# Gates of six column tiles by Strassen's form in a stage of their own, for all tokens

## The chip, the cores and the metric

The kernel runs on one core of a Trainium2 chip. A core has TensorE (PE, matrix products into PSUM banks), VectorE (DVE), ScalarE (ACT), GpSimd (POOL), SyncE (SP, which only issues DMAs here) and 16 DMA engines. The metric is the device time of one execution in microseconds (us); less is better.

## The reference

One encoder layer over 1024 tokens of width 1024, in fp32. Cut to what matters:

```python
mod = jax.nn.silu(c) @ w_ada + b_ada                      # six vectors of 1024
h = rmsnorm(x, norm1_g) * (1.0 + sc1) + sh1
z = h @ w_in
u, v, q, k, va, gate_a, gate_b = jnp.split(z, cuts, axis=-1)
a_out = gmlp_branch(u, v, gm_v_g, gm_w_s, gm_b_s) @ w_a   # 512 -> 1024
b_out = window_attention_branch(q, k, va, q_norm_g, k_norm_g, attn_sink) @ w_b
merged = jax.nn.sigmoid(gate_a) * a_out + jax.nn.sigmoid(gate_b) * b_out
x = x + gt1 * (merged @ w_o)
h2 = rmsnorm(x, norm2_g) * (1.0 + sc2) + sh2
f_gate, f_up = jnp.split(h2 @ w_ffn_in, 2, axis=-1)
x = x + gt2 * ((jax.nn.silu(f_gate) * f_up) @ w_ffn_out)
```

`gate_a` and `gate_b` are 1024 columns each of `h @ w_in`: the change is about these two products.

## The kernel before

**Products.** Matmuls take operands of type F32R; to keep fp32 accuracy every operand is split into a high and a low part, and every product is three matmuls (`mm3`: high x high, high x low, low x high) that accumulate in a PSUM bank of 128 x 512. A weight unit is 128 x 1024: `raw_unit` loads it (512 KB), `unit` casts it to `wh` on ScalarE and subtracts to `wl` on VectorE. `raw`, `wh` and `wl` have three buffers each.

**Stages.** Activations are held transposed (columns on partitions, tokens along the row), eight column tiles `d` or `k` of 128. Tokens run in two halves of 512: `half(0)`, `half(1)`. A half makes q and k (with `h`, the normalised input, of eight tiles), v, the attention with fillers between its steps (u and the gates of tiles 0 and 1), the spatial gating, and then two loops over `d`:

- The tile loop: the gates of tile `d` (for `d` > 1: two units `w_gb[d]`, `w_ga[d]`, 24 matmuls each), the projections of both branches with `w_ab[d]` (2 x 12 matmuls), sigmoid by tanh on ScalarE, the gated sum on VectorE and its split into `mH`, `mL`. Beside it run dot products for the conditioning vectors (`ada_next`: a `w_ada` unit of 512 KB times `silu_c` on VectorE with a sum, 1024 wide), and in half 0 loads of half 1's x with squares and their sum (`sumsq`), from which `col_rstd` takes the norms by four matmuls with ones.
- The output projection: 24 matmuls per tile with `w_o[d]`, the residual, x1 stored to `x1d`. In half 0 it also modulates x of half 1 to the `h` of half 1 (`h_next`), in half 1 x1 of half 0 to `h2`.

After both halves comes the FFN, already by Strassen's form, with an order written out by hand.

**What sets the order.** The Tile scheduler places instructions on each engine by their dependences; where `in_order[0]` is set they keep the program's order. Loads from SP (`load`) always keep the program's order among themselves, so a load that waits for its buffer holds all later loads. Stores go out on POOL's queue (`store`). Every operation of an engine is recorded at the helper's line L75; loads at L127, stores at L130.

**Buffers.** `stream("hs")` and `stream("xs")` are 128 x 512 with two buffers each; `midt` is 128 x 2048 with eight; `hid` 128 x 2048 with four; PSUM has four `mm` and four `at` banks.

Of the kernel before, what the change touches and what calls it, by code (L numbers as in the profile page):

```python
# [38 lines left out]
def kernel(  # L39
    ctx: ExitStack,  # L40
    tc: tile.TileContext,
    xT: bass.AP,
    c: bass.AP,
    cols: bass.AP,
# [47 lines left out]
    dram = ctx.enter_context(tc.tile_pool(name="dram", bufs=1, space=bass.MemoryType.DRAM))  # L92
    psum = ctx.enter_context(pool("psum", 4, space=PSUM))

    n_names = [0]
# [22 lines left out]
    def hid():  # L118
        return hpool.tile([P, 2048], F32R, tag="h", name=nm("h")).rearrange(
            "p (a b) -> p a b", a=4  # L120
        )

# [101 lines left out]


    apool_ctx = ExitStack()
    apool = apool_ctx.enter_context(pool("apool"))
    attp = apool_ctx.enter_context(pool("attp", 6))

    silu_c = apool.tile([P, D], F32, tag="silu_c", name="silu_c")  # L230
    rows = apool.tile([P, GW + 2 * HD + NH], F32, tag="rows", name="rows")
# [234 lines left out]

    EARLY = 6
    firsts, raw2 = {}, []
    ffn_ctx = ExitStack()
    fps = []  # L470

    def open_ffn():

        apool_ctx.close()
        fp = ffn_ctx.enter_context(pool("ffn"))
        fps.append(fp)
        for part in range(2):
            t = fp.tile([P, 2048], F32R, tag=f"b22{'hl'[part]}", name=nm("first"))
            firsts[part] = t

# [21 lines left out]

    def ada_next(n):
        for _ in range(n):
            if ada_queue:
                col, gain = ada_queue.pop(0)
                ada_dot(raw_unit(w_ada2[col - GT1]), col)
                ada_end(col, gain)

    def x_rows(hf, k):  # L510
        return xT[k * P : (k + 1) * P, hf * HALF : (hf + 1) * HALF]

    def half(hf):
# [62 lines left out]
        for k in range(KT):  # L576
            if hf == 0:
# [22 lines left out]
            elif k == 0:  # L600
                wq, wk = early.pop(0), early.pop(0)
            if k == 4:
                wk = unit(w_kv[1], V)
            if k % 2 == 1 and k < KT - 1:
                wq_next = unit(w_q[(k + 1) // 2], V)
            sts = [(hH[k // 4][:, k % 4, t * P : (t + 1) * P], hL[k // 4][:, k % 4, t * P : (t + 1) * P])
                   for t in range(NT)]
# [6 lines left out]
            for group in ((q_parts, k_parts) if k == 4 else (q_parts + k_parts,)):  # L614
                for e in range(2):
                    for ps, st, w, o, n, first, last in group:
                        if e == 0:
                            T.matmul(ps, st[0], w[0][:, o : o + n], start=k == 0 and first, stop=False)
                            T.matmul(ps, st[0], w[1][:, o : o + n], start=False, stop=False)
                        else:  # L620
                            T.matmul(ps, st[1], w[0][:, o : o + n], start=False,
                                     stop=bool(k == KT - 1 and last))
            if k % 2 == 1 and k < KT - 1:
                wq = wq_next
        in_order[0] = False
        if hf == 0:
            attention_constants()
        else:
            col_rstd(sums[0], NT, rcol[2])
        vts = {}  # L630
# [90 lines left out]


        vps = [mm_bank() for _ in range(NT)]
        wvs.append(unit(w_v[1], V))
# [64 lines left out]
        for s in range(nw):  # L789
            if s:  # L790
# [3 lines left out]
                den = exps(*sc, work[s][1])  # L794
            fill(FA)
            normalise(sc[0], sc[2], den)
            if s == 0:
# [60 lines left out]
        for ct in range(4):  # L858
# [3 lines left out]
            split(pt, gH[:, ct, :], gL[:, ct, :])  # L862

        mH = [None, None]
        mL = [None, None]
        for d in range(KT):
            if d % 4 == 0:
                mH[d // 4] = midt(F32R, 4)  # L870
                mL[d // 4] = midt(F32R, 4)
            ms = []
            in_order[0] = d < 2
            if d > 1:
                wg2 = unit(w_gb[d])
                wab = unit(w_ab[d])
                wg1 = unit(w_ga[d])
            else:
# [12 lines left out]
            split(ms[0], mH[d // 4][:, d % 4, :], mL[d // 4][:, d % 4, :])  # L891
            in_order[0] = False
            if d > 1:
                ada_next(2 + hf)
            if hf == 0:
                xk = stream("hs")
                load(xk, x_rows(1, d))
                if d == 0:
                    ssn = ss_tile()[:, :HALF]
                in_order[0] = d == 0  # L900
                sumsq(xk, d == 0, ssn)
                in_order[0] = False
        if hf == 0:
            col_rstd(ssn, NT, rcol[1])


        if hf == 1:
            assert not ada_queue
            open_ffn()
        dst = [[hid(), hid()], [hid(), hid()]]  # L910
        if hf == 0:
            h_next.extend(dst)
        else:
            h2[0] = dst
            x1B.extend([midt(F32, 4), midt(F32, 4)])
            h2m.extend([midt(F32, 4), midt(F32, 4)])
        ss = ss_tile()[:, :HALF]
        wo_next = unit(w_o[0])
        for d in range(KT):
            wo = wo_next  # L920
            if d < KT - 1:
                wo_next = unit(w_o[d + 1])
            elif hf == 0:
                early.extend([unit(w_q[0], V), unit(w_kv[0], V)])
            else:
                raw1 = raw_unit(w_gate[1])
                raw2.append(raw_unit(w_gate[2]))
# [3 lines left out]
            if hf == 1 and d in (2, 4):  # L931
                early.append(first_unit(d // 2 - 1))
            if hf == 0 and d in (2, 5):
                ada_next(1)
            xk = stream("hs")
            load(xk, x_rows(1, d) if hf == 0 else x1d[d * P : (d + 1) * P, :HALF])
            xr = stream("xs")
            load(xr, x_rows(hf, d))
            pw = mm_bank()
            for k in range(KT):  # L940
                kc = slice(k * P, (k + 1) * P)
                mm3(pw, (wo[0][:, kc], wo[1][:, kc]),
                    (mH[k // 4][:, k % 4, :], mL[k // 4][:, k % 4, :]), k == 0, k == KT - 1)
            if d == 0:
                rb = spread(rcol[1 + hf], NT)
            hi, lo = (t[d // 4][:, d % 4, :] for t in dst)
            modulate(xk, rb, d, SC1 if hf == 0 else SC2, SH1 if hf == 0 else SH2, hi, lo,
                     xk if hf == 0 else h2m[d // 4][:, d % 4, :])
            x1 = tmp() if hf == 0 else x1B[d // 4][:, d % 4, :]
            V.scalar_tensor_tensor(out=x1, in0=pw, scalar=mod[:, GT1 + d : GT1 + d + 1], in1=xr,  # L950
                                   op0=ALU.mult, op1=ALU.add)
            sumsq(x1, d == 0, ss)
            store(x1d[d * P : (d + 1) * P, hf * HALF : (hf + 1) * HALF], x1)
            if hf == 1 and d == KT - 1:
                early.append(unit(None, V, raw1))
        in_order[0] = False
        sums.append(ss)

    half(0)
    half(1)  # L960

    fp = fps[0]
    Q = HALF  # L970

    def fpt(name):
        return fp.tile([P, 2048], F32R, tag=name, name=nm(name)).rearrange("p (a b) -> p a b", a=4)

# [306 lines left out]
    with tc.manual_schedule():  # L1281
        U[4, 0], U[5, 0], U[0, 0], U[1, 0] = early
        buf = mid.tile([P, 2048], F32, tag="mid", name=nm("ws"))
        ws, ups = buf[:, :UNIT], (buf[:, UNIT:], fp.tile([P, UNIT], F32, tag="ru", name="ru"))
        g3 = gate_raw(3)
# [172 lines left out]
def _layout(inputs):  # L1458
# [10 lines left out]
    def col(v):  # L1469
# [9 lines left out]
    out = {  # L1479
        "xT": xt,  # L1480
        "c": a["c"][0],
        "cols": np.concatenate([col(a["b_ada"][0]), col(a["norm1_g"][0]), col(a["norm2_g"][0]),
# [39 lines left out]
```

## Time and profile before

| | us |
|---|---|
| median of three runs (lowest, highest) | 1257.36 (1256.26, 1259.01) |
| the profiled execution: span from first to last instruction | 1255.1 |
| TensorE busy in it | 1234.1 |
| VectorE, ScalarE, POOL busy | 861.5, 543.5, 132.7 |
| DMA queue of SP, of POOL | 155.59 MB, 57.68 MB |

The median lies 2.3 above the profiled span; the profiled execution's time beyond its span is not listed apart. Busy times are per engine and overlap. Rows of groups give the operation, output and inputs by the program's names, the shape, a count, the busy time, the mean in ns, and the idle time ahead of them with what ended it. A group's mean is the time from start to end of one instruction; in a dense row the next starts earlier, so prices are read from starts.

### The profile page before, as it was taken

Reading aid. Unit: us, or ns where it says so; the run is one execution under the profiler, and the core shown is the slowest. Engines: PE = TensorE matmul, PEld = TensorE weight load, DVE = VectorE, ACT = ScalarE, POOL = GpSimd, SP = SyncE. Lnnn points to the kernel's source line nnn. Section 1 sums busy time; section 2 is a strip of 40 time slices with the busy share of each in tenths; the row PEclk is TensorE's granted clock in tenths of the full one; section 3 lists DMA queues with packets and bytes.
Section 4 is the critical chain, followed back from the end, with each engine's and each line's share of the span. In section 5 each row is a group of like instructions: output and inputs, shape, how many; then the busy total and the mean of one; then the engine's idle time right before and its main releaser. Section 6 shows DMA issues by size and latency. Waiting matters only on the chain.

```text
span 1255.1 us, 15405 instructions
## 1 busy us (share of the span) xinstructions
PE 1234.1 (98%) x5714; PEld 1025.1 (82%) x5714; DVE 861.5 (69%) x1404; ACT 543.5 (43%) x867; POOL 132.7 (11%) x148
## 2 busy tenths in 40 slices
PE   5999999999999999999999999999999999999998
PEld 4888888888888888888888888888888887888887
DVE  8998875557468786666698766666666666455646
ACT  5467853334257772334454333333333334433342
POOL 0123310000032330000100000001010000010001
PEclk9999999999999999999999999999999999999999
DMA  9422145546522126665712454464554449896652
GB/s 362 169 84 67 52 143 184 177 159 211 197 70 67 51 89 196 201 194 209 250 36 102 147 189 151 154 213 182 205 189 180 168 168 357 280 328 187 196 161 101
DMA packets 67773, 214.25 MB, mean 171 GB/s; under 512 B 7793, under 2 KB 7793, under 8 KB 62450
## 3 DMA queue, kind: packets, MB, share of 16 engines
q1 hardware_dynamic: 56450, 155.59, 37.5%
q0 software_dynamic: 11248, 57.68, 12.7%
q8 instruction: 45, 0.74, 0.2%
q14 instruction: 30, 0.25, 0.1%
HBM read 170.24 MB, written 42.99 MB: 170 GB/s over the span
## 4 chain that ended last, share of the span: by engine, by line
PE 86%; DVE 6%; ACT 3%; DMA 3%; issue 1%; SPq 0%; POOL 0%; ACTq 0%; DVEq 0%
PE mm L75 47%; PE at L75 39%; DVE mid L75 2%; DVE wl L75 2%; ACT wh L75 1%; DMA mid<-in_w_ada_dram 1%; DMA hs<-in_xT_dram 1%; ACT lb L75 1%; DVE xs L75 0%; DMA mid<-in_xT_dram 0%; ACT mid L75 0%; DVE ws L75 0%; DMA raw<-in_w_o_dram 0%; DVE hid L75 0%; DMA raw<-in_w_q_dram 0%
## 5 line engine op out<-in xcount | busy, mean ns | idle before, releaser
L75 DVE TENSOR_TENSOR wl<-raw,wh 128x1024 fp32r<-128x1024 f32 x147 | 180.7, 1231 | 122.9 <-ACT wh L75 121.5
L75 ACT CAST wh<-raw 128x1024 fp32r<-128x1024 f32 x161 | 168.9, 1053 | 218.7 <-PE mm L75 126.7
L75 PE MATMUL mm<-mid,wh 128*128 128x512 f32 x736 | 227.8, 390 | 0.8 <-DVE mid L75 0.6
L75 PE MATMUL mm<-h,wh 128*128 128x512 f32 x608 | 187.9, 390 | 0.0
L75 PEld LDWEIGHTS mm<-mid,wh 128*128 128x128 f32 x736 | 137.7, 188 | 30.3 <-DVE mid L75 1.0
L75 PE MATMUL mm<-mid,wl 128*128 128x512 f32 x368 | 143.2, 389 | 0.0
L75 PEld LDWEIGHTS mm<-h,wh 128*128 128x128 f32 x608 | 113.7, 188 | 23.4
L75 PE MATMUL mm<-wh,h 128*128 128x512 f32 x384 | 129.7, 399 | 2.4 <-ACT h L75 2.3
L75 PE MATMUL mm<-h,wl 128*128 128x512 f32 x304 | 118.3, 389 | 0.0
L75 DVE TENSOR_TENSOR wl<-ws,wh 128x1024 fp32r<-128x1024 f32 (+1 forms) x55 | 62.0, 1128 | 43.6 <-ACT wh L75 43.6
L75 PEld LDWEIGHTS mm<-wh,h 128*128 128x128 f32 x384 | 71.7, 189 | 17.3 <-ACT h L75 3.2
L75 PEld LDWEIGHTS mm<-mid,wl 128*128 128x128 f32 x368 | 69.1, 188 | 14.4
L75 ACT CAST wh<-ws 128x1024 fp32r<-128x1024 f32 (+1 forms) x55 | 53.6, 974 | 58.6 <-DVE ws L75 42.1
L75 PE MATMUL mm<-wl,h 128*128 128x512 f32 x192 | 75.9, 395 | 0.0
L75 PE MATMUL at<-h,wh 128*128 128x512 f32 x240 | 74.1, 390 | 0.0
L75 PEld LDWEIGHTS mm<-h,wl 128*128 128x128 f32 x304 | 57.1, 188 | 12.0
L75 DVE SCALAR_TENSOR_TENSOR raw<-raw,silu_c 128x1024 f32<-128x1024 f32 x32 | 39.1, 1222 | 34.4 <-DMA raw<-in_w_ada_dram 33.5
L75 DVE TENSOR_TENSOR ol<-raw,oh 128x1024 fp32r<-128x1024 f32 x30 | 36.7, 1224 | 31.6 <-ACT oh L75 29.8
L75 ACT ACTIVATE xs<-xs 128x512 f32<-128x512 f32 x21 | 13.3, 633 | 96.4 <-DVE xs L75 96.4
L75 PE MATMUL at<-wl,wh 128*128 128x512 f32 x136 | 53.0, 390 | 0.7 <-DVE wl L75 0.7
L75 PE MATMUL at<-wh 128*128 128x512 f32 x136 | 53.0, 390 | 0.4 <-DVE mid L75 0.4
L75 PE MATMUL at<-wh,wl 128*128 128x512 f32 x136 | 52.9, 389 | 0.0
(244 smaller groups left out, 2459.8 us busy)
## 6 DMA issues: line engine op xcount, KB each, us to landing
raw<-in_w_ada_dram SPq DMA_DIRECT2D x32, 512.0 KB, 3.5
raw<-in_w_gate_dram SPq DMA_DIRECT2D x28, 512.0 KB, 4.1
tA<-hid POOLq DMA_DIRECT2D x11, 1024.0 KB, 5.0
tB<-hid POOLq DMA_DIRECT2D x11, 1024.0 KB, 4.9
wo<-in_w_out_dram POOLq DMA_DIRECT2D x22, 512.0 KB, 6.3
wS<-wo POOLq DMA_DIRECT2D x11, 1024.0 KB, 5.2
raw<-wS SPq DMA_DIRECT2D x44, 256.0 KB, 3.7
raw<-tB SPq DMA_DIRECT2D x44, 256.0 KB, 4.6
```

The costliest lines, as they stand in the source:

```text
L75: ins = f(*args, **kw)
```

## The change

- The gates of tiles 2 to 7 leave both halves' tile loops, which keep only the projections (24 matmuls per tile). For these tiles ScalarE copies the projections out of PSUM and POOL stores them to `pd` in DRAM (2 x 256 KB per tile and half); the merged tiles 0 and 1 are stored to `md`.
- Behind both halves' loops stands a gate stage: per tile, the 2 x 2 block product (two gates by two halves of the input columns, times these by two halves of tokens) in Strassen's form, seven products of 4 x 3 matmuls in place of eight. `GSTEP` lists them; three banks are in turn (two `mm`, one `at`). Product 6 of a tile comes behind product 0 of the next. Weight sums are made per tile (`gate_prep_a`, `_b`, `_c`), the branch results are read back (`branch_load`, 1 MB), gated and stored to `md`.
- The input's blocks (B11, B21, B22, T1, T3, T4, N2) are made in half 1's tile loop (`block_sums`) from rows that half 0 stores: x of half 0 scaled (`x0d`), and of half 1 (`x1sd`), four loads of 256 KB per chunk, into both buffers of `hs` and `xs`.
- Half 1's norms come from eight loads of rows of x with a square and sum on ScalarE (`x_square`), two in half 0's q/k phase and six in its attention; half 1's `h` is made in half 0's tile loop (`x_mod`).
- Both output projections follow the gate stage and read `md` back. The conditioning dots are spread anew: eight in half 0's tile loop, five in half 1's q/k phase, ten in the gate stage, five of them as two half rows, nine in the output projection of half 0.

In counts TensorE has 72 matmuls of 128x512 and four of 128x1 fewer, VectorE 87 operations more (77 of them sums of 128x512, five of 128x2048), ScalarE 55 more, POOL 54 stores of 256 KB more, SP 29 loads more.

TensorE before, at the border of two tiles in half 0's tile loop (`mid` are the branch's high and low parts, `h` the input's, `wh`, `wl` the units):

```order
888 L75 MATMUL mm_2106<-mid_760,wh_2028 128x512
889 L75 MATMUL mm_2106<-mid_761,wh_2028 128x512
890 L75 MATMUL mm_2106<-mid_760,wl_2029 128x512
891 L75 MATMUL mm_2156<-h_212,wh_2140 128x512
892 L75 MATMUL mm_2156<-h_214,wh_2140 128x512
893 L75 MATMUL mm_2156<-h_212,wl_2141 128x512
```

There the next tile's gate followed a projection. Now, in the gate stage, where `mid_3789` and `mid_3790` are the block B21 (high and low), `j_3850` and `j_3851` N2:

```order
1859 L76 MATMUL mm_4291<-mid_3789,wh_4241 128x512
1860 L76 MATMUL mm_4291<-mid_3790,wh_4241 128x512
1861 L76 MATMUL mm_4291<-mid_3789,wl_4242 128x512
1862 L76 MATMUL at_4365<-j_3850,wh_4321 128x512
1863 L76 MATMUL at_4365<-j_3851,wh_4321 128x512
1864 L76 MATMUL at_4365<-j_3850,wl_4322 128x512
```

One product follows another there, in another bank. VectorE before, in half 0's tile loop, with the gating of a tile (352, 354, 358), its split (356), splits of units (353, 357, 361) and dots (351, 359):

```order
351 L75 SCALAR_TENSOR_TENSOR raw_2361,acc_mod<-raw_2361,silu_c 128x1024
352 L75 SCALAR_TENSOR_TENSOR t_423_2222<-t_423_2222,mm_2224 128x512
353 L75 TENSOR_TENSOR wl_2269<-raw_2266,wh_2268 128x1024
354 L75 TENSOR_TENSOR t_420_2181<-t_420_2181,t_423_2222 128x512
355 L75 TENSOR_SCALAR mod<-acc_mod,cc 128x1
356 L75 TENSOR_TENSOR mid_2137<-t_420_2181,mid_2136 128x512
357 L75 TENSOR_TENSOR wl_2373<-raw_2370,wh_2372 128x1024
358 L75 SCALAR_TENSOR_TENSOR t_439_2297<-t_439_2297,mm_2299 128x512
359 L75 SCALAR_TENSOR_TENSOR raw_2473,acc_mod<-raw_2473,silu_c 128x1024
```

Now, in half 1's q/k phase behind that loop, with dots (356, 359) between the splits of half 1's q and k units:

```order
356 L76 SCALAR_TENSOR_TENSOR raw_2349,acc_mod<-raw_2349,silu_c 128x1024
357 L76 SCALAR_TENSOR_TENSOR mod<-acc_mod,badap,cc 128x1
358 L76 TENSOR_TENSOR wl_2300<-raw_2297,wh_2299 128x1024
359 L76 SCALAR_TENSOR_TENSOR raw_2382,acc_mod<-raw_2382,silu_c 128x1024
360 L76 SCALAR_TENSOR_TENSOR mod<-acc_mod,badap,cc 128x1
361 L76 TENSOR_TENSOR wl_2354<-raw_2351,wh_2353 128x1024
```

And VectorE in a period of the gate stage, with evictions of banks (725, 726, 729), splits of units (727, 733) and sums of weights:

```order
725 L76 TENSOR_TENSOR mid_4594<-at_4653,xs_4592 128x512
726 L76 TENSOR_TENSOR mid_4594<-mm_4619,mid_4594 128x512
727 L76 TENSOR_TENSOR wl_4672<-raw_4667,wh_4671 128x1024
728 L76 TENSOR_TENSOR t_931_4689<-raw_4669 128x512
729 L76 TENSOR_TENSOR mid_4594<-at_4653,mid_4594 128x512
730 L76 TENSOR_TENSOR raw_4669<-raw_4669,raw_4667 128x512
731 L76 TENSOR_TENSOR t_944_4758<-t_931_4689,t_943_4757 128x512
732 L76 TENSOR_TENSOR raw_4667<-raw_4667,t_931_4689 128x512
733 L76 TENSOR_TENSOR wl_4693<-raw_4669,wh_4692 128x1024
```

Where the gated sums stood between splits, the evictions of products do. SP before, the loads of one tile in the tile loop:

```order
61 L127 DMA hs_2365<-in_xT_dram 128x512
62 L127 DMA raw_2370<-in_w_gb_dram 128x1024
63 L127 DMA raw_2376<-in_w_ab_dram 128x1024
64 L127 DMA raw_2382<-in_w_ga_dram 128x1024
65 L127 DMA raw_2473<-in_w_ada_dram 128x1024
```

And now in the gate stage, where the read of the branch results stands ahead of the next tile's units:

```order
137 L137 DMA mid_4651<-pd 128x2048
138 L137 DMA raw_4667<-in_w_ga_dram 128x1024
139 L137 DMA raw_4669<-in_w_gb_dram 128x1024
140 L137 DMA raw_4712<-in_w_ada_dram 128x1024
141 L137 DMA hs_4719<-in_w_ada_dram 128x512
```

The core of the diff:

```diff
+    def x_square(i):
+        if i == 0:
+            next_x["ms"] = sm(8, "xms")
+        t, c = i // 2, i % 2
+        xk = stream("hs")
+        load(xk, xr[t * P : (t + 1) * P, c * 512 : (c + 1) * 512])
+        A.activation(xk, xk, AF.Square, accum_out=next_x["ms"][:, i : i + 1])
...
+    def block_load(k):
+        chunk = [stream(x) for x in ("hs", "hs", "xs", "xs")]
+        for i, src in enumerate((x0d, x1sd)):
+            for q in range(2):
+                load(chunk[2 * i + q], src[4 * q + k])
+        return chunk
...
+    GSTEP = ((0, 0, "B11", 0), (1, 0, "T3", 1), (0, 1, "B21", 0), (2, 0, "N2", 2),
+             (1, 1, "T4", 1), (3, 0, "T1", 2), (2, 1, "B22", 2))
+    def gate_step(d, i):
+        u, part, name, b = GSTEP[i]
+        first = i in (0, 1, 3)
+        if first:
+            acc[d, b] = at_bank() if b == 2 else mm_bank()
+        w, t, bank = gunits[d][u], blk[name], acc[d, b]
+        for k in range(4):
+            ks = slice(part * Q + k * P, part * Q + (k + 1) * P)
+            for j, (p, q) in enumerate(((0, 0), (0, 1), (1, 0))):
+                T.matmul(bank, w[p][:, ks], t[q][:, k, :], start=first and k + j == 0,
+                         stop=k == 3 and j == 2, skip_group_check=True)
...
+    def gate_evict(d, i):
+        bank, g, c = acc[d, GSTEP[i][3]], gate_t.get(d), base_t.get(d)
+        if i == 0:
+            base_t[d] = stream("xs")
+            A.copy(base_t[d], bank)
+            gate_t[d] = midt(F32, 4)
+        elif i == 2:
+            A.activation(g[:, 0, :], bank, AF.Tanh, scale=0.5)
+        else:
+            o = g[:, (3, None, 1, 1, 3, 2)[i - 1], :]
+            V.tensor_tensor(o, bank, o if i in (4, 5) else c, op=ALU.add)
+            if i > 3:
+                A.activation(o, o, AF.Tanh, scale=0.5 if i == 6 else -0.5)
...
+    def gating(d, hf=None, out=None):
+        g, b = gate_t[d], branch_t[d]
+        cs = slice(0, 4) if hf is None else slice(2 * hf, 2 * hf + 2)
+        V.scalar_tensor_tensor(out=g[:, cs, :], in0=g[:, cs, :], scalar=1.0, in1=b[:, cs, :],
+                               op0=ALU.add, op1=ALU.mult)
+        for h in range(2) if hf is None else (hf,):
+            o = g[:, 2 * h, :] if out is None or h else out
+            V.tensor_tensor(o, g[:, 2 * h, :], g[:, 2 * h + 1, :], op=ALU.add)
+            if out is None or h:
+                store(md[h][d], o)
...
-            if d > 1:
-                wg2 = unit(w_gb[d])
-                wab = unit(w_ab[d])
-                wg1 = unit(w_ga[d])
-            else:
-                wg1 = wg2 = None
-                wab = units[9 + d]
-            for (wg, o, br) in ((wg2, 512, (oH, oL)), (wg1, 0, (gH, gL))):
-                sg = gate_act(gate(wg)) if d > 1 else sgs.pop(0)
+            for br, t in ((1, (oH, oL)), (0, (gH, gL))):
                 pb = mm_bank()
                 for k in range(4):
-                    kc = slice(o + k * P, o + (k + 1) * P)
-                    mm3(pb, (wab[0][:, kc], wab[1][:, kc]),
-                        (br[0][:, k, :], br[1][:, k, :]), k == 0, k == 3)
-                V.scalar_tensor_tensor(out=sg, in0=sg, scalar=1.0, in1=pb, op0=ALU.add, op1=ALU.mult)
-                ms.append(sg)
-            V.tensor_tensor(ms[0], ms[0], ms[1], op=ALU.add)
-            split(ms[0], mH[d // 4][:, d % 4, :], mL[d // 4][:, d % 4, :])
+                    kc = slice(br * Q + k * P, br * Q + (k + 1) * P)
+                    mm3(pb, (wab[d][0][:, kc], wab[d][1][:, kc]), (t[0][:, k, :], t[1][:, k, :]),
+                        k == 0, k == 3)
+                if d < 2:
+                    sg = gates.pop(0)
+                    V.scalar_tensor_tensor(out=sg, in0=sg, scalar=1.0, in1=pb, op0=ALU.add,
+                                           op1=ALU.mult)
+                    ms.append(sg)
+                else:
+                    c = tmp()
+                    A.copy(c, pb)
+                    j = 2 * hf + br
+                    store(pd[d][:, j * Q : (j + 1) * Q], c)
+            if d < 2:
+                V.tensor_tensor(ms[0], ms[0], ms[1], op=ALU.add)
+                store(md[hf][d], ms[0])
             in_order[0] = False
-            if d > 1:
-                ada_next(2 + hf)
+            while jobs and jobs[0][0] <= d:
+                jobs.pop(0)[1]()
...
+    branch_load(2)
+    ada_half_load()
+    for d in range(2, KT):
+        last = d == KT - 1
+        gate_step(d, 0)
+        gate_evict(d, 0)
+        if d > 2:
+            gate_step(d - 1, 6)
+        gate_prep_c(d)
+        if d > 2:
+            gate_evict(d - 1, 6)
+        gate_step(d, 1)
+        gate_evict(d, 1)
+        gate_step(d, 2)
+        gate_evict(d, 2)
+        if d > 2:
+            if last:
+                m0.extend(m_tiles(midt))
+                for k in range(2):
+                    m_load(m0, 0, k)
+                m_src[6] = tmp()
+                gating(d - 1, None, m_src[6])
+            else:
+                gating(d - 1)
+        if not last:
+            branch_load(d + 1)
+        gate_step(d, 3)
+        gate_evict(d, 3)
+        if not last:
+            gate_load(d + 1)
+            gate_prep_a(d + 1)
+        else:
+            wo_next = unit(w_o[0])
+            for k in (0, 1):
+                m_split(m0, k)
+                m_load(m0, 0, k + 2)
+        gate_step(d, 4)
+        gate_evict(d, 4)
+        if not last:
+            gate_prep_b(d + 1)
+        else:
+            m_split(m0, 6)
+            for k in (2, 3):
+                m_split(m0, k)
+                m_load(m0, 0, k + 2)
+            m_src[7] = tmp()
+            gating(d, 0, m_src[7])
+        gate_step(d, 5)
+        gate_evict(d, 5)
+        if d == 2:
+            ada_load()
+        else:
+            ada_next(not last)
+        if not last:
+            ada_half(d < KT - 2)
```

More of the change, by code (lines that the diff above doesn't have):

```diff
@@ L467 @@
     EARLY = 6
+    Q = HALF
     firsts, raw2 = {}, []
[L469 to L479, printed above, removed]
     def first_unit(i):
@@ L501, with ada_load, ada_next @@
     )
[L503 to L508, printed above, removed]
+    ada_ahead = []
+    def ada_load():
+        if ada_queue:
+            col, gain = ada_queue.pop(0)
+            ada_ahead.append((col, gain, raw_unit(w_ada2[col - GT1])))
+    def ada_next(more=True):
+        if not ada_ahead:
+            return
+        col, gain, r = ada_ahead.pop(0)
+        ada_dot(r, col)
+        ada_end(col, gain)
+        if more:
+            ada_load()
@@ L915, in half, with mod2 @@
+    for k in (4, 5, 7):
+        m_split(m0, k)
+    gate_step(KT - 1, 6)
+    gate_evict(KT - 1, 6)
+    gating(KT - 1, 1)
+    m = m0
+    ada_load()
+    for hf in range(2):
+        if hf == 1:
+            h2[0] = [[hid(), hid()], [hid(), hid()]]
             x1B.extend([midt(F32, 4), midt(F32, 4)])
             h2m.extend([midt(F32, 4), midt(F32, 4)])
+            for part in range(2):
+                firsts[part] = flat(jt(F32R, 4))
         ss = ss_tile()[:, :HALF]
-        wo_next = unit(w_o[0])
+        def mod2(d):
+            xk = stream("hs")
+            load(xk, x1d[d * P : (d + 1) * P, :HALF])
+            hi, lo = (t[d // 4][:, d % 4, :] for t in h2[0])
+            modulate(xk, rb, d, SC2, SH2, hi, lo, h2m[d // 4][:, d % 4, :])
@@ L932, in half @@
                 early.append(first_unit(d // 2 - 1))
[L933 to L938, printed above, removed]
+            xk = stream("xs")
+            load(xk, x_rows(hf, d))
             pw = mm_bank()
```

276 lines of the change are left out of this document (235 added, 41 removed).

## The prediction

> **What bounds the kernel now.** I read the page's busy times and its chain first, then the waits of TensorE after the start, then one call of stage windows where the change works.
>
> ```profile
> span 1255.1 us, 15405 instructions
> PE 1234.1 (98%) x5714; PEld 1025.1 (82%) x5714; DVE 861.5 (69%) x1404; ACT 543.5 (43%) x867; POOL 132.7 (11%) x148
> ...
> PEclk9999999999999999999999999999999999999999
> ...
> PE 86%; DVE 6%; ACT 3%; DMA 3%; issue 1%; SPq 0%; POOL 0%; ACTq 0%; DVEq 0%
> ```
>
> TensorE is busy 98% of the span at full clock, and 86% of the chain that ends last is its own work. The waits of TensorE between 60 and 1250 us are all short:
>
> ```profile
> PE mm L75 <- DVE mid L75: 1.0, 2, 0.6
> PE at L75 <- DVE wl L75: 0.7, 1, 0.7
> PE at L75 <- DVE nmx L75: 0.6, 2, 0.3
> PE at L75 <- DVE mid L75: 0.4, 1, 0.4
> PE mm L75 <- DVE xs L75: 0.2, 1, 0.2
> ```
>
> That is 2.9 us in 1190 (total, times, longest). So behind the start, time is the number of matmuls times their spacing: a matmul taken out shortens the end, and a new wait lengthens it one for one. The windows of the two tile loops and one of the FFN (columns: PE, PEld, DVE, ACT, POOL, clock, DMA share, GB/s):
>
> ```profile
> 175.00:200.00 25.00, 25.00 (x112) 20.68 (x111) 17.91 (x29) 8.65 (x13) 0.00 (x0) 1.00 0.57 180
> 225.00:250.00 25.00, 25.00 (x112) 20.71 (x111) 15.65 (x24) 9.03 (x12) 0.00 (x0) 1.00 0.60 191
> 525.00:550.00 25.00, 25.00 (x112) 20.71 (x111) 14.30 (x24) 6.93 (x9) 0.00 (x0) 1.00 0.65 206
> 1050.00:1075.00 25.00, 25.00 (x112) 20.70 (x111) 13.21 (x11) 13.62 (x15) 0.00 (x0) 1.00 1.04 389
> ```
>
> The loops have no TensorE idle to win back, but VectorE has 7 to 11 of each 25 us free and the DMA engines some 40%. The FFN window shows TensorE undisturbed at 389 GB/s.
>
> **The change part by part. TensorE.** The group means (390 ns) overlap; spacing is what counts. Starts in the loop of half 0:
>
> ```profile
> 170.05 0.61 PE L75 MATMUL mm<-mid,wh 128*128 128x512 f32 x2
> 170.50 0.39 PE L75 MATMUL mm<-mid,wl 128*128 128x512 f32 x1
> 170.73 0.61 PE L75 MATMUL mm<-mid,wh 128*128 128x512 f32 x2
> ```
>
> Three matmuls take 170.73 − 170.05 = 0.68 us, 0.2267 each. Gates of six tiles were 2 halves x 2 units x 24 = 96 matmuls per tile and are 7 x 12 = 84: 6 x 12 = 72 fewer, 72 x 0.2267 = **−16.3 us**. TensorE's order shows matmuls of the same shape in both, so the price holds. The four 128x1 matmuls that go too are left at nothing.
>
> Everything else moves under TensorE, so the question is what now comes late. Durations, by starts in a dense stretch of VectorE (its ends overlap the next start):
>
> ```profile
> 177.58 1.22 DVE L75 TENSOR_TENSOR wl<-raw,wh 128x1024 fp32r<-128x1024 f32 x1
> 178.71 0.68 DVE L75 TENSOR_TENSOR mid<-t,mid 128x512 fp32r<-128x512 f32 x1
> 179.31 0.68 DVE L75 SCALAR_TENSOR_TENSOR t<-t,mm 128x512 f32<-128x512 f32 x1
> 179.91 0.68 DVE L75 TENSOR_TENSOR ss<-ss,t 128x512 f32<-128x512 f32 x1
> 180.51 0.20 DVE L75 TENSOR_SCALAR mod<-acc_mod,cc 128x1 f32<-128x1 f32 x1
> ...
> 181.23 1.22 DVE L75 SCALAR_TENSOR_TENSOR raw<-raw,silu_c 128x1024 f32<-128x1024 f32 x1
> 182.38 0.08 DVE L75 DVE_READ_ACCUMULATOR raw<-raw,silu_c 128x1 f32 x1
> ```
>
> So 0.60 for 512 columns, 1.13 for 1024, 1.23 for an ada dot with its read, 0.13 for a small one. A 2048-wide operation does not occur before; by the step from 512 to 1024 (0.53 per 512) I take 1.13 + 2 x 0.53 = 2.2, ends 2 x 1.13 = 2.3 and 4 x 0.60 = 2.4. ScalarE and the DMA:
>
> ```profile
> L75 ACT CAST wh<-raw 128x1024 fp32r<-128x1024 f32 x161 | 168.9, 1053 | 218.7 <-PE mm L75 126.7
> L75 ACT ACTIVATE xs<-xs 128x512 f32<-128x512 f32 x21 | 13.3, 633 | 96.4 <-DVE xs L75 96.4
> raw<-in_w_ada_dram SPq DMA_DIRECT2D x32, 512.0 KB, 3.5
> raw<-in_w_ga_dram SPq DMA_DIRECT2D x16, 512.0 KB, 4.0
> hs<-in_xT_dram SPq DMA_DIRECT2D x16, 256.0 KB, 3.9
> hs<-x1d SPq DMA_DIRECT2D x8, 256.0 KB, 5.6
> tA<-hid POOLq DMA_DIRECT2D x11, 1024.0 KB, 5.0
> mid<-in_w_ada_dram SPq DMA_DIRECT2D x8, 1024.0 KB, 9.0
> ```
>
> **Attention of half 0** gets six squares with a sum on ScalarE, 0.63 plus a read of the sum, some 0.8 each, 5 us in about 100. ScalarE is busiest there, and a late exponential holds the next transpose:
>
> ```profile
> 125.00:150.00 25.00, 24.73 (x131) 20.85 (x130) 20.98 (x59) 20.16 (x47) 9.66 (x6) 1.00 0.13 43
> ```
>
> 20.16 of 25 leaves room; 0 to 1.5, I take 0.4. The column sums that go cost nothing visible.
>
> **Loop of half 0**: only projections remain, 24 x 0.2267 = 5.44 us per tile, 43.5 for eight, where 16.3 per tile stood. Into these go eight dots (8 x 1.36), eight pairs of modulating operations (16 x 0.66, from the row quoted for half 1), eight weight splits (8 x 1.13) and the first two tiles' gating (6 x 0.60): 34 of VectorE's 43.5. The DMAs weigh more: 15 loads of 512 KB, 8 of 256 KB, and 22 stores of 256 KB by POOL are 15 x 0.524 + 30 x 0.262 = 15.7 MB, 361 GB/s, against 180 to 191 before. At the window's 389 it takes 40.4 of 43.5. It fits, with 3 us to spare and three weight buffers; in VectorE's order a dot (row 359) stands ahead of a split of half 1's weights (row 361), so a late dot holds that unit and then TensorE. With landings of 3.5 to 4.5 nothing is late; each further us counts more than once through the buffers. 0 to 4, I take 1.0. [...]
>
> **Half 1's q/k phase** gets five dots (5 x 1.36) between its splits; 0 to 1, I take 0.3.
>
> **Loop of half 1** makes the blocks. Per chunk, seven operations of 0.60 and four with a column of scalars:
>
> ```profile
> L75 DVE SCALAR_TENSOR_TENSOR h<-mid,mod,h 128x512 fp32r<-128x512 f32 x16 | 11.9, 746 | 3.3 <-ACT h L75 3.2
> ```
>
> 746 ns against the 0.68 above makes 0.60 + 0.06 = 0.66 for those: 6.8 per chunk, 27.4 for four. With six weight splits (6.8), the first gate unit and half of the second (3.5) and gating (3.6) VectorE has 41.3 of 43.5, 2.2 spare. A chunk is four loads of 256 KB that fill both buffers of `hs` and `xs`, so the next is issued only when the last operation has read them; two splits (2.3) and a little more lie under the landing, about 2.7. Three reloads cost 3 x (L − 2.7) − 2.2: nothing at L = 3.0, 1.4 at 3.9, 6.5 at 5.6. It is held up at the entry of the gate stage, where steps 1 and 3 want units behind the block work. I take the row of loads from DRAM of the same shape, 3.9: 1.5; ends 0 and 7.
>
> **Gate stage.** In TensorE's order, as the section on the change shows it, one product of 12 follows another with the banks in turn. A bank is left for one product (12 x 0.2267 = 2.72 us) between its uses. A period is 84 x 0.2267 = 19.05. In VectorE's order of one period the evictions (rows 725, 726, 729) stand between splits. A tile has three splits (3.4), five sums and one short split of weights (5 x 0.60), five evictions (3.0), the gating (2.2 and 2 x 0.60), a dot and two half dots (1.23 + 1.4) and small ones (0.6): 16 of 19.05. An eviction that waits behind one split is late by 1.1 and still inside 2.72. The tighter chain is the load. The read of `pd` (row 137 of SP's order) is for tile d+1 and waits for a buffer that the gating of tile d−1 frees, and all loads of the next weights queue behind it. The gating runs after product 6 (5.44), its eviction, tanh and a split: some 7.4 to 9.7 of the period. Then the read (1 MB, 5.0 by the row of `tA`) and the gate unit (4.0) come: side by side the unit is there at 13.7, one after the other at 18.7; I take the middle, 16. Cast and split (1.05 + 1.13) then end at 18.2, needed at 19.05: slack 0.8. The late end would cost 1.9 in each of five periods, 9 in all; by the middle nothing or a little, and I take 0.8 in all. The end of the stage and the output projections, where TensorE's order has seven matmuls ahead of the last product, 0 to 2: 0.5.
>
> Sum: −16.3 + 0.4 + 1.0 + 0.3 + 1.5 + 0.8 + 0.5 = −11.8. On the profiled span, 1255.1 − 11.8 = 1243.3; the median lies 2.3 above that span (1257.4), so **1245.6**.
>
> **The rivals.**
> *No new wait*: every cover holds; VectorE's 34, 41 and 16 all lie below TensorE's time, and before, all covers held to 2.9 us. 1257.4 − 16.3 = 1241.1. Chance 0.13.
> *Both loops become bound by transfers*: for it stand 361 GB/s and the fully used buffers; against it the 389 of the FFN at full TensorE. At the upper ends (4 + 7, with the other terms 2.0) the sum is −3.3: 1254; half of that, 1250. Chance 0.16.
> *The gate stage is bound by its load chain, slower*: if the raw unit takes 9.0 us (the row of 1 MB loads in a full queue) and not 4.0 behind the read of `pd`, each of five periods loses 5.0 − 0.8 = 4.2, 21 in all: 1245.6 − 0.8 + 21 = 1266. It decides from (11.8 + 0.8)/5 + 0.8 = 3.3 us more, a landing of 7.3. Against it: the stage's demand is 1 MB of `pd`, four units of 512 KB and two stores of 256 KB, 3.7 MB in 19 us or 193 GB/s, and at 180 to 206 GB/s gate units landed in 4.0. Idle TensorE has a further price, seen at the start:
>
> ```profile
> 22.77 0.79 PE L75 MATMUL mm<-wh,h 128*128 128x512 f32 x1 [1.77 <-ACT h L75]
> 23.36 0.63 PE L75 MATMUL mm<-wl,h 128*128 128x512 f32 x1
> 23.78 0.63 PE L75 MATMUL mm<-wh,h 128*128 128x512 f32 x1
> 24.21 0.63 PE L75 MATMUL mm<-wl,h 128*128 128x512 f32 x1
> ```
>
> There matmuls stand 0.43 apart, not 0.227, while the granted clock reads full; eight of them cost 1.6 more. If each long stall brought that, the five periods would lose 8 more: 1274. [...] Chance of the rival, with and without it, 0.16.
>
> **How the numbers follow.** Forecast 1245.6, chance 0.55, its own range 1242 to 1250; the rivals 0.13, 0.16 and 0.16. The range to hold 8 in 10 runs from no wait (1240.5, some measurement spread below 1241.1) to the loops' upper ends, 1256. About 0.2% (2.5 us) is what a measurement of this kernel tells from no change: the three runs spread by 2.7. Faster than 1254.9: 0.55 + 0.13 + 0.11 of the second rival = 0.79; within 0.2%: its remaining 0.05; slower: 0.16.
>
> **What would show it.** Right: TensorE's busy time lower by about 16 and its waits up by 3 to 6, split between the entry of the gate stage (`wl` behind block sums, those behind `hs`) and the end of half 0's loop; DMA share near 0.9 in the loops; in the gate stage 112 matmuls per 25 us. Wrong: fewer than 108 there, waits for raw gate units or for `pd`; matmuls 0.43 apart behind the start; or the attention of half 0 longer by more than 2 us.

## The result, and the profile after

The changed kernel takes 1274.06 us (median of four, 1270.48 to 1275.74) against 1257.09 before: 1.0127 times as long, 95% interval 1.011 to 1.0144. Forecast were 1245.6 us, 1240.5 to 1256, with a chance of 0.16 for slower. It is 28 us above the forecast. The profiled execution is the fastest of the four, 1270.48 us with a span of 1268.7, 13.6 longer than that of before; what the others lose on top was not broken down.

The page after, the rows that answer to those of before:

```profile
span 1268.7 us, 15580 instructions
PE 1234.8 (97%) x5634; PEld 1014.8 (80%) x5634; DVE 911.9 (72%) x1496; ACT 572.5 (45%) x930; POOL 161.1 (13%) x202
```

TensorE has 80 recorded matmuls fewer (72, and the four of 128x1 with two records each) and is as long busy as before, 1234.8 against 1234.1. So 16 us of matmuls went and as much busy time came back: matmuls took longer. Beside that its waits behind 165 us (totals, times, longest):

```profile
PE at L76 <- DVE wl L76: 4.7, 4, 3.3
PE mm L76 <- DVE wl L76: 3.5, 4, 2.4
PE at L76 <- DVE ss L76: 3.2, 1, 3.2
PE mm L76 <- ACT t L76: 1.9, 2, 1.2
PE at L76 <- DVE mid L76: 1.1, 2, 0.7
PE mm L76 <- ACT wh L76: 0.9, 1, 0.9
PE mm L76 <- ACT xs L76: 0.4, 1, 0.4
PE mm L76 <- DVE mid L76: 0.4, 1, 0.4
PE at L76 <- DVE nmx L76: 0.3, 1, 0.3
```

They sum to 16.4, where 2.6 stood behind 165 us before: 13.8 us more. The rest is in two places that the waits do not show. The first are windows with a granted clock under 1.00 (the column behind POOL):

```profile
200.00:225.00 25.00, 19.82 (x80) 15.78 (x79) 14.23 (x22) 9.61 (x15) 5.37 (x10) 0.89 0.86 301
225.00:250.00 25.00, 24.79 (x131) 21.14 (x131) 9.12 (x14) 4.10 (x4) 0.00 (x0) 0.97 0.58 188
400.00:425.00 25.00, 24.07 (x97) 18.77 (x95) 19.85 (x32) 11.85 (x18) 1.96 (x4) 0.93 0.75 276
575.00:600.00 25.00, 21.85 (x96) 17.64 (x95) 14.60 (x20) 10.21 (x13) 3.25 (x5) 0.93 0.75 244
```

0.07 of 25 us at half clock is a stretch of 3.4 us, and 0.11 and 0.03 together one of 6.8: three stretches, 13.7 us at half speed, 6.8 us lost. Before had none behind its start. The second is the spacing of matmuls that read the new `j` tiles, in the FFN, whose matmuls and their order the change leaves alone; its `tt1`, `tt2` and `b22` tiles now come from the pool `j`:

```profile
849.61 0.40 PE L76 MATMUL at<-j,wh 128*128 128x512 f32 x1
849.85 0.39 PE L76 MATMUL at<-j,wl 128*128 128x512 f32 x1
850.08 0.63 PE L76 MATMUL at<-j,wh 128*128 128x512 f32 x2
850.55 0.40 PE L76 MATMUL at<-j,wl 128*128 128x512 f32 x1
850.78 0.63 PE L76 MATMUL at<-j,wh 128*128 128x512 f32 x2
```

Three take 850.78 − 850.08 = 0.70, not 0.68. By starts of all such pairs it is 232.8 ns against 227, 1248 matmuls (840 in the FFN, 216 in the gate stage, 192 in the output projection of half 1), about 7.5 us. From stage starts in the two traces, set side by side (ideal is the count times 0.2267):

| stage | before | after | ideal after |
|---|---|---|---|
| tile loop, half 0 | 108.9 | 45.2 | 43.5 |
| output projection, half 0 | 45.6 | 47.9 (later) | 46.2 |
| half 1 up to its tile loop | 137.4 | 144.1 | |
| tile loop, half 1 | 109.8 | 47.9 | 43.5 |
| gate stage | | 116.9 | 111.5 |
| output projection, half 1 | 44.5 | 51.4 | 43.8 |
| FFN to the last matmul | 636.2 | 642.6 | 631.1 |

The books: −16.3 + 13.8 + 6.8 + 7.5 = 11.8, of 13.6; 1.8 us were not traced further.

### The profile page after: what moved, and what is told of

Same layout as the page of the kernel before. It is cut to its first block, busy times and chain, and to the rows that moved or that the text cites. A ratio compares the mean times of both kernels' runs of the same rounds, so it can differ in the third digit from the quotient of the medians.

```text
span 1268.7 us, 15580 instructions
## 1 busy us (share of the span) xinstructions
PE 1234.8 (97%) x5634; PEld 1014.8 (80%) x5634; DVE 911.9 (72%) x1496; ACT 572.5 (45%) x930; POOL 161.1 (13%) x202
## 4 chain that ended last, share of the span: by engine, by line
PE 60%; issue 13%; DMA 11%; DVE 10%; ACT 5%; POOL 1%; SPq 0%; DVEq 0%; ACTq 0%; POOLq 0%
PE at L76 31%; PE mm L76 28%; DVE mid L76 3%; DVE wl L76 2%; DMA raw<-in_w_ada_dram 2%; DMA raw<-in_w_o_dram 2%; DMA raw<-in_w_ab_dram 2%; ACT wh L76 1%; ACT lb L76 1%; ACT mid L76 1%; DVE raw L76 1%; DMA mid<-in_w_ada_dram 1%; DVE xs L76 1%; DMA wo<-in_w_out_dram 1%; DMA hs<-md 1%
## 5 line engine op out<-in xcount | busy, mean ns | idle before, releaser
L76 DVE TENSOR_TENSOR wl<-raw,wh 128x1024 fp32r<-128x1024 f32 x141 | 172.0, 1221 | 89.2 <-ACT wh L76 85.6
L76 PE MATMUL at<-j,wh 128*128 128x512 f32 x464 | 145.5, 394 | 0.0
L76 PEld LDWEIGHTS at<-j,wh 128*128 128x128 f32 x464 | 87.1, 188 | 20.5
L76 DVE TENSOR_TENSOR wl<-ws,wh 128x1024 fp32r<-128x1024 f32 (+1 forms) x55 | 62.0, 1127 | 44.5 <-ACT wh L76 44.5
L76 PE MATMUL at<-j,wl 128*128 128x512 f32 x232 | 91.8, 395 | 0.5 <-DVE wl L76 0.5
L76 PE MATMUL mm<-j,wh 128*128 128x512 f32 x288 | 91.6, 399 | 0.0
L76 PE MATMUL at<-h,wh 128*128 128x512 f32 x288 | 89.1, 390 | 0.7 <-DVE mid L76 0.7
L76 PE MATMUL mm<-h,wh 128*128 128x512 f32 x272 | 84.6, 392 | 0.0
L76 PEld LDWEIGHTS mm<-j,wh 128*128 128x128 f32 x288 | 54.7, 190 | 12.6
L76 PEld LDWEIGHTS at<-h,wh 128*128 128x128 f32 x288 | 53.8, 188 | 12.2 <-DVE mid L76 1.1
L76 PEld LDWEIGHTS mm<-h,wh 128*128 128x128 f32 x272 | 50.6, 188 | 10.5
```

What stands on the lines that cost most here:

```text
L76: ins = f(*args, **kw)
```

## The experiments

**The spacing.** The new constant `shd` moves all later tiles by 32 bytes, so the first guess was that offset. Two kernels, one from each side:

```diff
-    shd = const.tile([P, 8], F32, tag="shd", name="shd")
+    shd = const.tile([P, 16], F32, tag="shd", name="shd")
```

> The changed kernel with its new constant tile of 8 columns (32 bytes a partition) padded to 16 (64 bytes), so that every later tile starts on a multiple of 64 bytes as before the change; nothing else moves. Theory A (the 32-byte offset slows matmuls that read the `j` tiles): matmuls with `j` operands stand 227 ns apart instead of 233, the FFN takes 636 us instead of 643 as before the change, the span falls by 8 to 10 us. Rival B (it is the `j` pool itself, its place or its bookkeeping): 233 ns and 643 us stay, the time changes by less than 1 us. The half-clock stretches stay in both.

The spacing stays 232.8 ns, the FFN 641.9, the ratio to before is 1.0112 (1.009 to 1.0134). And the offset put into the kernel before:

```diff
+    pad = const.tile([P, 8], F32, tag="pad", name="pad")
+    V.memset(pad, 0.0)
```

> The kernel before with an unused constant tile of 8 columns (32 bytes) added, which moves every later tile by 32 bytes; one tiny instruction more, all else the same. Theory A (offset): matmuls that read the `tt1`, `tt2`, `b22` tiles of the FFN go from 227 to about 233 ns, some 800 matmuls or 5 us, others by 0 to 1 ns; the time rises by 5 to 8 us. Rival B (the `j` pool): spacing stays 227 and the time stays within 1 us of before.

1.0005 (0.9995 to 1.0014), FFN 636.4. The offset is not it. The built programs show another difference. In the kernel before, `mid`, `h`, `wh`, `wl` and the FFN's own tiles all start at the same remainder modulo 2048 bytes, 1216, and still at one remainder with the pad. Three small tiles of the change (`xms`, `part`, `xs4`, four buffers of 32 bytes each) put `j` 384 bytes off the others, with and without the wider `shd`.

```diff
-            next_x["ms"] = sm(8, "xms")
+            next_x["ms"] = sm(8, "ms")
...
-        part = sm(1, "part")
+        part = sm(1, "ms")
...
-        s = sm(4, "xs4")
+        s = sm(4, "ms")
```

> The changed kernel with its three new small tiles put under a tag that exists (no new buffers, 384 bytes less), so that the `j` tiles start at the same remainder modulo 2048 bytes as `mid`, `h`, `wh` and `wl`, as the FFN's tiles did before; 32 bytes of the new constant stay. Theory G (matmuls whose two operands lie at different remainders stand further apart): matmuls with `j` go from 233 to 227 ns, the FFN from 642.6 to 636 us, the gate stage and the second output projection by 1 to 1.5 us each, 8 to 9 us in all. Rival B (the `j` pool itself): 233 ns and 642.6 us stay, under 1 us.

Theory G holds for the spacing: 226.9 ns, the FFN 637.6. The mean of a row falls with it. After, then this kernel:

```profile
L76 PE MATMUL at<-j,wh 128*128 128x512 f32 x464 | 145.5, 394 | 0.0
```

```profile
L76 PE MATMUL at<-j,wh 128*128 128x512 f32 x464 | 142.9, 389 | 0.0
```

The time is 1266.48, ratio 1.0073 (1.0055 to 1.0092). The 8 to 9 us in all did not come: the span falls by 4.3. The FFN takes 5.0 less, but the gate stage (117.7) and the second output projection (51.9) take 0.8 and 0.5 more. Two periods of the gate stage without a stall do fall, from 19.3 to 19.1, but this run has 17.1 us of half clock behind 165 us where the changed kernel had 13.7, a new stretch of 3.4 in the gate stage among them. And in the kernel before, where only the tiles placed behind the pad move:

```diff
+    pad = small.tile([P, 96], F32, tag="pad", name="pad", bufs=1)
+    V.memset(pad[:, :8], 0.0)
```

> The kernel before with an unused tile of 384 bytes ahead of the FFN's tiles (`b22`, `tt1`, `tt2`), which then start at another remainder modulo 2048 bytes than `h` and the weights; `mid`, `h`, `wh` and `wl` stay where they are. Theory G: matmuls with these tiles go from 227 to about 233 ns, 800 of them and more, the FFN from 636 to 641 or 642 us, the time 5 to 6 us up. Rival B: 227 ns and within 1 us of before.

1.0044 (1.0029 to 1.0059), 5.5 us; the FFN takes 642.3, the change's loss there within 0.4. The windows of before and of this kernel, the same 100 us:

```profile
900.00:1000.00 100.00, 100.00 (x443) 82.77 (x442) 67.60 (x94) 33.09 (x46) 7.51 (x14) 1.00 0.52 184
```

```profile
900.00:1000.00 100.00, 100.00 (x436) 81.55 (x436) 64.65 (x90) 33.96 (x47) 7.64 (x15) 1.00 0.54 187
```

Seven matmuls fewer fit, TensorE 100% busy and at full clock in both: only a count shows it. Three more kernels, with pads of 128, 32 and 64 columns and one execution each, ask for the modulus:

> The kernel before with 512 bytes ahead of the FFN's tiles in place of 384. If a remainder modulo 512 bytes decides the spacing, it is 227 ns there and the FFN takes 636 us; if the modulus is larger (1024 or 2048), 232 ns or more and 641 or 642 us.

> The kernel before with 128 bytes ahead of the FFN's tiles. If the modulus is 128 bytes or less the spacing stays at 227 ns, which the 384 bytes (three times 128) speak against; otherwise it grows, by less than 5 ns if the distance matters by degrees, to 232 ns if any difference does.

> The kernel before with 256 bytes ahead of the FFN's tiles. 512 bytes left the spacing at 227 ns, 128 and 384 made it 232. If the modulus is 512 bytes: 232 ns and an FFN of 641 or 642 us here too; if it is 256: 227 ns and 636 us.

The FFN takes 636.2 us with 512 bytes, 641.8 with 128 and 637.0 with 256 (whole executions 1258.33, 1261.80 and 1256.64). The row that reads weights from such a tile, for 128 and for 256 bytes:

```profile
L75 PE MATMUL mm<-h,first 128*128 128x512 f32 x24 | 5.9, 395 | 0.0
```

```profile
L75 PE MATMUL mm<-h,first 128*128 128x512 f32 x24 | 5.8, 389 | 0.0
```

Where the moved tile is the moving operand (`b22h` with `wl`, 88 matmuls) the means are 395 with 128 and 384 bytes and 389 with 256, 512 and before. So 128 and 384 bytes cost 6 ns a matmul here, 256 and 512 nothing, whether the moved tile holds the moving operand or the weights. A smaller step than 128 between operands was not tried.

**The entry of half 1.** VectorE after, where TensorE waited 3.3 us at 220:

```profile
210.20 1.23 DVE L76 TENSOR_TENSOR wl<-raw,wh 128x1024 fp32r<-128x1024 f32 x1 [0.40 <-ACT wh L76]
217.83 1.22 DVE L76 SCALAR_TENSOR_TENSOR raw<-raw,silu_c 128x1024 f32<-128x1024 f32 x1 [6.41 <-DMA raw<-in_w_ada_dram]
218.99 0.08 DVE L76 DVE_READ_ACCUMULATOR raw<-raw,silu_c 128x1 f32 x1
218.99 1.22 DVE L76 TENSOR_TENSOR wl<-raw,wh 128x1024 fp32r<-128x1024 f32 x1
```

A dot waits 6.4 us for its load, behind it the split of the k unit, whose cast had ended at 213.2. That dot follows the split in the program; the scheduler put it ahead.

```diff
+            in_order[0] = True
             early.append(unit(None, V, early_raw[1]))
+            in_order[0] = False
...
+                was, in_order[0] = in_order[0], True
                 wq_next = unit(w_q[(k + 1) // 2], V)
+                in_order[0] = was
...
+                in_order[0] = True
                 ada_next(k < 7)
+                in_order[0] = False
```

> The changed kernel with VectorE's order fixed at the entry of half 1: the splits of its first q and k units keep the program's order with the conditioning dots, so no dot stands ahead of them. Theory C (the stall of 3.7 us at 220 us and the half-clock stretch behind it come from the dot that waits 6.4 us for its load ahead of the split): both go, half 1's phase and attention fall from 144 to 137 or 138 us, 6 to 7 us less in all. Rival D (the transfers of the whole loop are late, so the next unit takes the dot's place): the stall moves to the next split and at most 2 us are won.

1263.83, ratio 1.0053 (1.0037 to 1.0069). Half 1 up to its tile loop falls from 144.1 to 138.0, as theory C has it. Its tile loop and the gate stage together take 1.5 more (166.4): there a wait of 2.7 us, with 6.8 us of half clock, stands where 2.4 with 3.4 stood. In its trace the split waits for its cast alone:

```profile
212.12 1.22 DVE L76 TENSOR_TENSOR wl<-raw,wh 128x1024 fp32r<-128x1024 f32 x1 [1.80 <-ACT wh L76]
214.08 1.23 DVE L76 TENSOR_TENSOR wl<-raw,wh 128x1024 fp32r<-128x1024 f32 x1 [0.73 <-ACT wh L76]
215.60 1.23 DVE L76 SCALAR_TENSOR_TENSOR raw<-raw,silu_c 128x1024 f32<-128x1024 f32 x1 [0.30 <-DMA raw<-in_w_ada_dram]
```

**The sums in half 1's output projection.** TensorE's column sums of half 0's x1 wait for VectorE, where the last addition stands behind the split of a late `w_o` unit:

```profile
579.72 1.05 PE L76 MATMUL at<-ones,ss 128*128 128x1 f32 x8 [3.15 <-DVE ss L76]
```

```diff
-                if d == 0:
+                if d == 1:
                     col_rstd(sums[0], NT, rcol[2])
-                elif d == 1:
+                elif d == 2:
                     rb = spread(rcol[2], NT)
-                if d:
+                    mod2(0)
+                if d > 1:
                     mod2(d - 1)
```

> The changed kernel with the column sums of half 0's x1 and their spread one tile later in the second output projection. Theory E (TensorE's ones-matmul waits 3.5 us for the last sum, which stands on VectorE behind the split of a late `w_o` unit, and the half clock follows): stall and half-clock stretch at 580 us go, the second output projection falls from 51.4 to 46 or 47 us, 4 to 5 us in all. Rival F (the `w_o` unit itself is late and TensorE would wait for it anyway): the stall becomes a wait for `wl` or `wh` at the same place and less than 2 us are won.

The projection falls from 51.4 to 46.4, as theory E has it; 1264.88 (two executions), ratio 1.0062 (1.0042 to 1.0082). The window there runs at full clock again:

```profile
575.00:600.00 25.00, 25.00 (x117) 20.59 (x116) 17.41 (x22) 10.90 (x14) 3.72 (x5) 1.00 0.82 279
```

**Half 1's tile loop.** After, between 380 and 405 us, ScalarE waits for the chunk, VectorE for ScalarE, TensorE for a split queued behind that:

```profile
ACT mid L76 <- DMA hs<-x0d: 7.2, 4, 2.6
DVE mid L76 <- ACT mid L76: 5.7, 4, 3.1
...
PE mm L76 <- DVE wl L76: 2.4, 1, 2.4
```

```diff
-                if part and k < 3:
-                    chunk[0] = block_load(k + 1)
```

> The changed kernel without the three reloads of the chunk in half 1's tile loop: the blocks of chunks 1 to 3 are made from what the first chunk left in its buffers, 12 loads of 256 KB are left out, every instruction of an engine stays. Theory H (landings of the reloads, on VectorE and ScalarE, make the stalls at the loop's end and the gate stage's entry, some 2.5 us each and the half clock behind): half 1's loop falls from 47.9 to 44, the gate stage from 116.9 to 113 or 114, 6 to 8 us in all. Rival I (VectorE's work itself, 41 of 43.5 us, is late): less than 2 us.

The window from 375 to 400 us after, then without the reloads:

```profile
375.00:400.00 25.00, 22.64 (x100) 18.46 (x99) 17.64 (x26) 14.45 (x23) 3.98 (x8) 1.00 0.77 256
```

```profile
375.00:400.00 25.00, 25.00 (x112) 20.71 (x111) 25.00 (x37) 18.19 (x29) 4.86 (x9) 1.00 0.58 177
```

The loop falls from 47.9 to 43.7, the gate stage from 116.9 to 115.3: 5.9 us, just under theory H's 6 to 8, and 1.7 of it is the half clock at 400 us that goes too. The one execution took 1265.73. VectorE is busy throughout the window, but TensorE does not wait for it, so VectorE's work by itself is not late. The kernel leaves out the landings and their 3.1 MB of transfers at once; which of the two counts is not separated.

**The three mends together**

> The changed kernel with the three edits together: the dots behind the splits at the entry of half 1, the column sums of half 0 a tile later, and the three small tiles without buffers of their own. If each mends what it is thought to and nothing else comes late, 6.1 + 5.0 + 8.5 us go from the changed kernel: about 1252, which is faster than the kernel before by 4 to 5 us. If theory G falls, about 1261, slower than before. If the stalls only move to the gate stage's entry (1.6 and 3.1 us were seen there with the first edit), 2 to 4 us more than these.

1253.85 (1249.64 to 1258.71, ten executions), 0.998 of before (0.9967 to 0.9992): 2 to 3 us under the kernel before, and 1.9 above the 1252 expected. The executions spread by 9 us, and why was not found; the profile is that of the fastest, 1249.64. It has TensorE 1219.1 busy, 15.0 less than before, no half clock between 165 and 1240, and these waits of over 1 us in total behind 165:

```profile
PE mm L76 <- DVE wl L76: 3.7, 4, 1.8
PE at L76 <- DVE mid L76: 1.5, 2, 1.1
PE mm L76 <- ACT t L76: 1.2, 2, 0.8
PE at L76 <- DVE wl L76: 1.1, 2, 0.7
PE mm L76 <- ACT wh L76: 1.1, 1, 1.1
```

Some of them lie where splits stand behind chunk rows. Off VectorE with those:

```diff
-                wab.append(unit(None, V, abr.pop(0)))
+                wab.append(unit(None, G if hf and d > 3 else V, abr.pop(0)))
...
-                gate_prep_a(2)
+                gate_prep_a(2, G)
```

> The kernel with the three edits, and with three splits of half 1's tile loop (the projection units of tiles 6 and 7 and the first gate unit) on POOL, 2.4 us each there, so that they no longer stand on VectorE behind block rows that wait for a chunk. Theory H (what is left of stall at the loop's end and the gate stage's entry, 1.4 and 1.9 us, comes from splits queued behind late chunk rows): both go, half 1's loop and the gate stage together fall from 163.4 to about 160, 3 us less. Rival J (the blocks themselves, T3 above all, are late, so the stall stays as a wait for a block): less than 1 us; with POOL's stores to DRAM behind the splits a wait for `t` may even cost 1 us.

1260.11, 1.0017 (1.0007 to 1.0027), worse than without. The largest wait is now another one:

```profile
PE mm L76 <- ACT wh L76: 5.3, 2, 4.7
PE mm L76 <- ACT t L76: 2.7, 4, 0.9
...
PE mm L76 <- POOL wl L76: 1.2, 1, 1.2
```

The loop and the gate stage take 169.8 in place of 163.4, 3.4 of it by a half-clock stretch of 6.8: TensorE waits 1.2 for a split on POOL, and 4.7 at the gate stage's entry for the cast of a gate unit, which itself waits for VectorE's sum of its weights. Why this sum comes late was not followed. Rival J has the sign, though not the place.

## Why the prediction was wrong

The profiled span is 1268.7 where the sum gave 1243.3. Of these 25.4 us, 7.5 are the spacing of matmuls on `j`, 6.8 the half clock, 9.3 waits beyond the 4.5 that the sum had for them, and 1.8 were not traced. The median lies 5.4 above its profiled span in place of 2.3, which makes up the rest of the 28.

**TensorE, −16.3: right in count, wrong in price.** The sentence that failed is "matmuls of the same shape in both, so the price holds". 72 matmuls went, but 1248 of the others came to stand 6 ns further apart, two thirds of them in the FFN, where the change only takes their tiles from another pool. The place of tiles in SBUF was no term of the sum, and no trace of before could price it: there the operands of these products all started at one remainder.

**Half 0's loop and the entry of half 1, 1.0 and 0.3.** The mechanism was named (a dot ahead of a split, a late load) and the ends were 0 to 5; the loop lost 1.7 against its ideal and half 1 up to its tile loop 6.7 against before, by a wait of 3.3, the half clock behind it (3.4) and smaller waits. The rate was mis-sized too: the loop moves 322 GB/s at a share of 0.94, or 343 at a share of 1.00 if the rate goes with the share (an estimate),

```profile
175.00:200.00 25.00, 25.00 (x112) 20.70 (x111) 19.54 (x34) 8.75 (x12) 5.40 (x10) 1.00 0.94 322
```

where I took the FFN's 389, which stood at a share of 1.04. The loops' own rows before point lower: by the same estimate 180 GB/s at 0.57 is 316 at 1.00, 206 at 0.65 is 317. By 317 the loop's 15.7 MB would need 49.5 us, by 343 they need 45.8, not 40.4 of 43.5; the loop took 45.2. The landing of a dot's unit, by its row of DMA issues, went from 3.5 to 5.5:

```profile
raw<-in_w_ada_dram SPq DMA_DIRECT2D x27, 512.0 KB, 5.5
```

The one that counted landed 6.3 after its issue, and VectorE stood 6.4 for it. But the loop itself lost only 1.7. The order made most of the price: with the dot behind the split 6.1 of the 6.7 went.

**Half 1's loop, 1.5 (0 to 7):** 5.9 by the kernel without the reloads, inside the ends. The mechanism was right and the landing mis-sized: the last load of each reload landed 5.8, 5.9 and 4.5 us after its issue, not 3.9. By their mean, 5.4, the formula gives the same 5.9, in part by luck, since 1.7 of the measured 5.9 is half clock, which it did not have.

**Gate stage, 0.8:** 5.4 over its ideal. Of it 216 matmuls on `j` are 1.3, the entry behind the chunk 1.7 (it goes without the reloads), and one of five periods paid the late end that was worked out, here 1.5 of wait: its first unit was cast 7.9 us after its load was issued, where 4.0 was taken for the landing. The other periods kept their cover. So the rival that was forecast for "slower" had the sign by another way, and that its 1274 is the measured median is luck.

**Output projections, 0.5:** the second alone 6.9. The sum's wait was missed, since I looked at the seven matmuls at the gate stage's end and not at what else had moved behind a busy queue: `col_rstd` of half 0 used to run behind half 1's q/k phase, 31 us after its projection had ended, and now comes one tile after it. The kernel with the sums a tile later wins 5.0 of the 6.9.

**The half clock** was priced in the rival alone, for a long stall that would repeat in each period. Three single waits of 2.4 to 3.3 us brought it, 6.8 us on top of 8.8 of wait. The start's rows had matmuls 0.43 apart behind a wait of 1.77; two of the same shape ahead of that wait (at 19.80 and 20.37 us) stood 0.57 apart, so what the wait itself cost there was not shown, and the sum had no term for it. Two of the named signs of being wrong came: matmuls 0.43 apart behind the start, and 102 matmuls in the gate stage's window from 475 to 500.

## What to carry to other kernels

Price a transfer-heavy stage by the windows of the same stage, GB/s over DMA share, not by the best window of the kernel: here 317 stood nearer than 389 to the 343 of the changed loop (322 at 0.94). Where a change adds tiles, ask what moves in SBUF behind them, and count matmuls per window in a stage that should not have changed (437 in the FFN's 100 us here, where 443 stood before). Behind 165 us, the waits of TensorE of 3.3, 2.4 and 3.2 us in the changed kernel and of 4.7 with splits on POOL were each followed by half clock, which cost 1.7 or 3.4 us on top, so order a slow consumer of a load (a dot, a sum) behind the splits that TensorE needs next.

## What the runs showed of the hardware

Matmuls of 128x512 that read `j`, which starts 384 bytes off the weights (modulo 2048), stood 232.8 ns apart in the changed kernel, 226.9 once `j` was moved back. With the FFN's tiles moved in the kernel before, the FFN took 642.3 us at 384 bytes and 641.8 at 128, but 637.0 at 256 and 636.2 at 512, where it took 636.2 unmoved.

The half clock came in stretches of 3.4 or 6.8 us, one of them without a long idle. In the kernel with the small tiles alone two waits of 1.0 and 0.5 us on either side of a few matmuls brought one, and the matmuls behind stand 0.43 apart:

```profile
482.14 0.73 PE L76 MATMUL mm<-mid,wh 128*128 128x512 f32 x2 [1.01 <-ACT wh L76]
483.40 0.50 PE L76 MATMUL mm<-mid,wl 128*128 128x512 f32 x1 [0.53 <-DVE wl L76]
...
484.71 1.05 PE L76 MATMUL mm<-mid,wh 128*128 128x512 f32 x2
485.56 0.63 PE L76 MATMUL mm<-mid,wl 128*128 128x512 f32 x1
```

With the same pair in the changed kernel (0.9 and 0.5 us, at 483) and with a single wait of 1.8 in the three mends no stretch followed. The half clock of the changed kernel sets in at 219.6, 400.5 and 581.5 us, 180.9 apart, and its clock records between start and end last 6.827, 174.080, 3.413, 177.493, 3.413 and 682.666 us: 2, 51, 1, 52, 1 and 200 times 3.413. Counted on this grid in that trace behind 165 us, over windows that began at full clock, the three with 2.7, 2.1 and 1.7 us of idle TensorE were followed by half clock, the next three, with 1.5, 1.4 and 1.2, were not, and none below. The wait of 3.2 us at 576.6 lies across two of these windows, 1.5 in the first and 1.7 in the second, so in this trace it mattered where a wait fell. What decides among the short waits, such as the 1.0 and 0.5 above, was not found.
